# Mixer input normalized before its split, accumulators copied out by ScalarE, weights split by ScalarE and VectorE

## The chip, the cores and the metric

The kernel runs on one core of one Trainium2 chip. The metric is the device time of one execution in microseconds (us), of which the median over several runs is given. The core's engines are TensorE (PE in the profile; its weight loads are PEld), VectorE (DVE), ScalarE (ACT), GpSimd (POOL) and SyncE (SP), which issues the transfers. Each works through its own queue in order.

## The reference

One step of a decoder layer over 1024 prompt positions and 8 decode positions, 1032 rows of 1024 features. The mixer projects the normalized input once; the columns are q, k and v of three attention patterns, the gate z, the convolved inputs xBC and dt of a state space branch. Both branches go through one output projection, and a SwiGLU block follows.

```python
def rmsnorm(x, w):
    xf = x.astype(jnp.float32)
    y = xf * lax.rsqrt(jnp.mean(xf * xf, axis=-1, keepdims=True) + NORM_EPS)
    return (y * w.astype(jnp.float32)).astype(x.dtype)
...
    qkv, z, xbc, dt_raw = split_mix(xn @ w_in)
...
    mix = jnp.concatenate([attn.astype(xn.dtype), ssm.astype(xn.dtype)], axis=-1) @ w_out
...
    yp = yp + rmsnorm(mix, norm_mix_post[l])
    yp = yp + rmsnorm(swiglu(rmsnorm(yp, norm_ffn_pre[l]), w_ffn_in[l], w_ffn_out[l]), norm_ffn_post[l])
```

## The kernel before

Features lie on the 128 partitions (8 tiles of 128, index `k`), the 1032 rows on the free axis in three chunks of 344 (`CH`). Every product is made of parts in TensorE's fp32r type: an operand `x` is split into a rounded high part `xh` and the rest `xl`, a weight tile into `wh` and `wl`, and `unit` (L161) adds `wh*xh`, `wl*xh` and `wh*xl` over the 8 tiles: 24 matmuls of 344 columns into one accumulator in PSUM. `gemm` (L182) loads one weight tile of 128 output features, runs a unit for each chunk and hands each accumulator to an evacuation function `ev`.

`load_w` (L136) brings a tile of 128 x 1024 weights from HBM (`wr`) and splits it. `wr`, `wh` and `wl` have two buffers each, so a tile's split waits until TensorE has left the tile before the last, and a transfer into `wr` until the low part of the tile before the last is made. The first load is split by GpSimd in quarters (L146, L148). The others go to GpSimd (L156, L158), but for four loads of the last chunk of the output projection (`share`, L153, L154), which ScalarE and VectorE split. Some further weights (the attention part of the output projection, one FFN tile, the last FFN group) have splits of their own on ScalarE and GpSimd.

The stages in order of time: the mixer's input; xBC columns (`w_in` tiles 44 to 55) with a convolution, and dt (to some 200 us); then q, k, v columns of the three patterns (`proj_raw`, L580) with attention beside the state space scan, and scores against the caches (200 to 900); z columns and the gate, with the merge of the patterns (L844 to L858) and the values of the caches (L861 to L889) beside them; the output projection and two norms (to some 1210); the FFN in four groups of hidden tiles; the last norm.

The mixer's input (L200 to L233) is only scaled by the norm's weights before the split: ScalarE writes `xh` from the loaded chunk `xc` with one scaled copy (L217), VectorE makes `xl` (L218). The row scale `rin`, one over the root mean square, is worked out beside the products: squares on ScalarE (L228), their sum over `k` on VectorE or GpSimd (L230), one product with a matrix of ones (L232) and `rms` (L190): a root on ScalarE and a reciprocal on VectorE. As the row scale is the same for all features of a row, it is multiplied in when an accumulator is copied out: `scaled` (L237, the multiplication in L239) on VectorE for xBC (`xb`), dt (`dtT`), q, k, v (`rw`) and z (`zt`). The first two weight tiles run as six units with six accumulators.

Accumulators of the mixer's columns have two slots in PSUM (six for the xBC columns). The order of instructions on each queue is made ahead of time by a scheduler that takes ready instructions by priority: `evac` before `w` (weights) before `side` before `late` before `main` (the matmuls of units). On the chip each queue keeps that order.

Of the kernel before, what the change touches and what calls it, by code (L numbers as in the profile page):

```python
# [48 lines left out]
def trunk(tc, a, o):  # L49
# [86 lines left out]
    def load_w(src, cols, share=False, kind="w"):  # L136
        with prio(kind):
# [5 lines left out]
            if nload[0] == 1:  # L143
                for q in range(4):
                    qs = slice(q * 256, (q + 1) * 256)
                    nc.gpsimd.tensor_scalar(out=wh[:, qs], in0=wr[:, qs], scalar1=1.0, scalar2=0.0, op0=ALU.mult,  # L146
                                            op1=ALU.add)
                    nc.gpsimd.tensor_tensor(out=wl[:, qs], in0=wr[:, qs], in1=wh[:, qs], op=ALU.subtract)  # L148
            elif share == 2:
                nc.scalar.copy(wh[:, :cols], wr[:, :cols])  # L150
                nc.gpsimd.tensor_tensor(out=wl[:, :cols], in0=wr[:, :cols], in1=wh[:, :cols], op=ALU.subtract)
            elif share and nload[0] % 2:
                nc.scalar.copy(wh[:, :cols], wr[:, :cols])  # L153
                nc.vector.tensor_tensor(out=wl[:, :cols], in0=wr[:, :cols], in1=wh[:, :cols], op=ALU.subtract)  # L154
            else:
                nc.gpsimd.tensor_scalar(out=wh[:, :cols], in0=wr[:, :cols], scalar1=1.0, scalar2=0.0,  # L156
                                        op0=ALU.mult, op1=ALU.add)
                nc.gpsimd.tensor_tensor(out=wl[:, :cols], in0=wr[:, :cols], in1=wh[:, :cols], op=ALU.subtract)  # L158
# [43 lines left out]
    # mixer input scaled by its norm's weights, split into two exact parts; its row scale is applied after the product  # L202
    xh = [actp.tile([P, T], F32R, tag="act", name=f"xh{k}") for k in range(KT)]
    xl = [actp.tile([P, T], F32R, tag="act", name=f"xl{k}") for k in range(KT)]
    rin = rowp.tile([P, T], F32, tag="row", name="rin")
    with ExitStack() as ps0:
        xp = pool(ps0, "xp", 3, side="left")
        sp = pool(ps0, "sqp", 3, side="left")
        xcs = []
        cuts = []  # L210
        for c, (c0, c1) in enumerate(CH):
            xc = xp.tile([P, KT, CW], F32, tag="xc", name="xc")
            xcs.append(xc)
            with prio("evac"):
                for k in range(KT):
                    nc.sync.dma_start(out=xc[:, k], in_=a["xT"][k, :, c0:c1])
                    cut = nc.scalar.activation(out=xh[k][:, c0:c1], in_=xc[:, k], func=AF.Copy, scale=nw(MIX_PRE, k))  # L217
                    nc.vector.scalar_tensor_tensor(out=xl[k][:, c0:c1], in0=xc[:, k], scalar=nw(MIX_PRE, k),  # L218
                                                   in1=xh[k][:, c0:c1], op0=ALU.mult, op1=ALU.subtract)
            cuts.append(cut)  # L220
            if c == 0:
                first.append(load_w(a["w_in"][45], 1024, kind="evac"))
        for c, (c0, c1) in enumerate(CH):
            acc = sp.tile([P, CW], F32, tag="acc", name="acc0")
            with prio("w"):
                for k in range(KT):
                    sq = acc if k == 0 else sp.tile([P, CW], F32, tag=f"sq{c % 2}", name="sq")
                    after(nc.scalar.activation(out=sq, in_=xcs[c][:, k], func=AF.Square), cuts[c])  # L228
                    if k:
                        (nc.vector if c == 1 else nc.gpsimd).tensor_tensor(out=acc, in0=acc, in1=sq, op=ALU.add)  # L230
                ssq = side_ps("ssq")
                nc.tensor.matmul(ssq[:, :CW], ones, acc, start=True, stop=True)  # L232
                rms(ssq[:, :CW], rin[:, c0:c1])  # L233
# [68 lines left out]
    # xBC columns, causal convolution  # L302
# [4 lines left out]
    for m in range(12):  # L307
# [4 lines left out]
        def ev(c, ps, xb=xb):  # L312
            c0, c1 = CH[c]
            return scaled(xb[:, 3 + c0:3 + c1], ps, c, rin)
# [46 lines left out]
    # dt: both parts of the weights side by side, then token-major  # L361
# [4 lines left out]
    for c, (c0, c1) in enumerate(CH):  # L366
# [5 lines left out]
        with prio("evac"):  # L372
            scaled(dtT[:, c0:c1], ps[:32], c, rin)
# [10 lines left out]
    with prio("side"):  # L384
# [43 lines left out]
        # decode step of the state space branch  # L428
# [44 lines left out]
    # chunked scan of the state space branch  # L473
    hst = sc.tile([P, 2, 512], F32, name="hst")

    def ssd(c, g):
# [42 lines left out]
        # outputs with features on partitions, two heads on each tile  # L519
# [36 lines left out]
    # y kept with its decode columns for the gate  # L556
    with prio("side"):
        nc.sync.dma_start(out=y_d[:, :, S:T].rearrange("k p b -> p k b"), in_=yd)
    # attention
# [20 lines left out]
    def proj_raw(mt):  # L580
        rw = rawp.tile([P, T], F32, tag="raw", name="rw")

        def ev(c, ps, rw=rw):
            c0, c1 = CH[c]
            return scaled(rw[:, c0:c1], ps, c, rin)
# [43 lines left out]
    def attend(g, hp, qr, kr, vt):  # L629
        nh = nhp.tile([P, S], F32, tag="nh", name="nh")  # L630
        for j in range(8):
# [43 lines left out]
            # features on partitions, the two heads side by side in the array  # L675
# [45 lines left out]
    # attention of the decode tokens over the caches  # L721
# [8 lines left out]
    def dec_scores(g):  # L730
        nc.vector.tensor_tensor(out=prod[:, g], in0=dec[0][:, g].rearrange("p h b -> p (h b)"),
                                in1=dec[1][:, g].rearrange("p h b -> p (h b)"), op=ALU.mult)
        # rows of the decode tokens: q for the scores, k and v for the new cache rows
# [79 lines left out]
    # merge of the three patterns by their softmax denominators  # L813
# [46 lines left out]
    # values of the caches  # L860
# [31 lines left out]
    # z columns and the gate  # L892
# [4 lines left out]
    for k in range(KT):  # L897
        zt = gp.tile([P, T], F32, tag="zt", name="zt")

        def ev(c, ps, zt=zt):  # L900
            c0, c1 = CH[c]
            return scaled(zt[:, c0:c1], ps, c, rin)
# [34 lines left out]
    # output projection: state space part, its row scale applied after the product  # L937
# [46 lines left out]
    # output projection: attention part, then both norms around the residual  # L984
# [57 lines left out]
    # SwiGLU in groups of hidden tiles  # L1042
# [23 lines left out]
    def ffn_in(ts, order):  # L1066
        """hidden tiles ts; order: (tile, chunk) one after the other"""
# [24 lines left out]
    def ffn_out(gi):  # L1092
# [15 lines left out]
        # the last group chunk by chunk, its weights and the residual on chip  # L1108
# [40 lines left out]
        for c, (c0, c1) in enumerate(CL):  # L1149
# [5 lines left out]
            with prio("side"):  # L1155
                for m in range(KT):
# [7 lines left out]
                    # two tiles to a transfer, in columns that have gone out  # L1164
# [8 lines left out]
    for gi, (t0, t1) in enumerate(groups):  # L1173
        if gi == 0:
            # the last chunk of the first two tiles late, while its norms are under way
# [98 lines left out]
```

## Time and profile before

| | |
|---|---|
| median of 3 runs | 1947.85 us (1947.51 to 1948.57) |
| span of the profiled execution | 1955.3 us |
| TensorE busy | 1827.1 us (93%) |
| VectorE busy | 1071.0 us (55%) |
| GpSimd busy | 856.4 us (44%) |
| ScalarE busy | 549.2 us (28%) |
| TensorE's granted clock, mean | 0.970 |

The profiled execution took a little longer than the runs that are timed. Busy time of TensorE counts matmuls with their modelled ends, which overlap, so it says that the engine had work, not that it ran at its peak. The granted clock is the share of full speed that TensorE was given: 1.00 is 2.4 GHz, 0.50 is 1.2 GHz, a mean between them is a mixture. A wait is put down to the instruction that released it last. In the rows, `L158` is line 158 of the kernel, `wl<-wr,wh` names what is written from what, and `g` is an accumulator.

### The profile page before, as it was taken

The page shows a single profiled execution, that of the slowest core. Times are in us where ns is not written, and L with a number is a line of the kernel's source. Part 1 is how long each engine was busy: PE and PEld are TensorE (multiplying, and loading weights), DVE is VectorE, ACT ScalarE, POOL GpSimd, SP SyncE. Part 2 cuts the span into 40 slices and gives each one's busy share as a digit, 9 for nine tenths or more (in the row PEclk, how much of TensorE's full clock was granted, in tenths as well). Part 3 has the DMA queues.
Part 4 walks back from the last instruction along what each step waited for, and adds up shares of the span by engine and source line. Part 5 has one row for each costly group of instructions (what it writes and reads, how often), then busy time and mean ns, then how long its engine had stood idle before and what let it go on. Part 6 is the DMA issues. An engine that isn't in the chain of part 4 may idle for free.

```text
span 1955.3 us, 29265 instructions
## 1 busy us (share of the span) xinstructions
PE 1827.1 (93%) x11685; PEld 1712.4 (88%) x11685; DVE 1071.0 (55%) x1917; ACT 549.2 (28%) x1084; POOL 856.4 (44%) x557
## 2 busy tenths in 40 slices
PE   7999989999999999998789889999999999999994
PEld 7998777888887898886678879999999999999993
DVE  7866776768774554556884796330233223321348
ACT  5322344343533344452231334111111001100142
POOL 6332356665435534356755564223223332233325
PEclk9999999999999999999889999999999999999997
DMA  5322333443324433365554444236533753355362
GB/s 188 114 92 87 111 110 100 126 127 110 117 83 153 161 99 104 130 233 150 154 158 130 134 134 151 97 128 244 178 108 103 253 172 119 119 202 196 116 251 87
DMA packets 125545, 275.27 MB, mean 141 GB/s; under 512 B 17616, under 2 KB 83632, under 8 KB 124000
## 3 DMA queue, kind: packets, MB, share of 16 engines
q1 hardware_dynamic: 125408, 273.39, 42.8%
q8 instruction: 92, 1.51, 0.3%
q14 instruction: 45, 0.37, 0.1%
HBM read 235.86 MB, written 125.47 MB: 185 GB/s over the span
## 4 chain that ended last, share of the span: by engine, by line
PE 39%; DVE 7%; DMA 2%; issue 1%; POOL 1%; ACT 1%; DVEq 0%; SPq 0%; POOLq 0%; ACTq 0%
PE g L169 14%; PE pu L169 12%; PE pg L169 12%; DMA nt<-n_d 1%; DVE mix L1030 1%; DVE fl L1033 1%; PE g L954 1%; DVE nt L856 1%; DVE nt L855 1%; DMA xr<-in_xT 0%; DVE mix L1029 0%; POOL nt L854 0%; DVE fr L192 0%; DVE nr L192 0%; DVE sl L924 0%
## 5 line engine op out<-in xcount | busy, mean ns | idle before, releaser
L169 PE MATMUL g<-xh,wh 128*128 128x344 f32 x1344 | 446.0, 332 | 32.4 <-DVE rw L239 12.7
L169 PE MATMUL g<-xl,wh 128*128 128x344 f32 x1344 | 443.2, 330 | 2.8 <-DVE xl L218 2.7
L169 PE MATMUL g<-xh,wl 128*128 128x344 f32 x1344 | 441.9, 329 | 1.9 <-POOL wl L158 1.2
L156 POOL TENSOR_SCALAR wh<-wr 128x1024 fp32r<-128x1024 f32 (+1 forms) x133 | 140.4, 1056 | 674.5 <-PE g L169 355.8
L158 POOL TENSOR_TENSOR wl<-wr,wh 128x1024 fp32r<-128x1024 f32 (+1 forms) x133 | 312.8, 2352 | 9.8
L169 PEld LDWEIGHTS g<-xh,wh 128*128 128x128 f32 x1344 | 258.1, 192 | 46.4 <-issue 14.4
L169 PEld LDWEIGHTS g<-xh,wl 128*128 128x128 f32 x1344 | 258.1, 192 | 11.5 <-issue 7.5
L169 PEld LDWEIGHTS g<-xl,wh 128*128 128x128 f32 x1344 | 258.0, 192 | 11.0 <-issue 6.1
L239 DVE TENSOR_TENSOR u<-pu,rf 128x344 f32<-128x344 f32 x66 | 34.0, 515 | 237.5 <-PE pu L169 237.5
L169 PE MATMUL pg<-fh,wh 128*128 128x344 f32 x504 | 158.8, 323 | 4.9 <-DVE mix L1010 4.9
L169 PE MATMUL pg<-fl,wh 128*128 128x344 f32 x504 | 162.1, 322 | 0.0
L169 PE MATMUL pu<-fl,wh 128*128 128x344 f32 x504 | 161.8, 321 | 0.0
L169 PE MATMUL pg<-fh,wl 128*128 128x344 f32 x504 | 161.4, 320 | 0.0
L169 PE MATMUL pu<-fh,wh 128*128 128x344 f32 x504 | 161.0, 319 | 0.0
L169 PE MATMUL pu<-fh,wl 128*128 128x344 f32 x504 | 160.4, 318 | 0.0
L169 PE MATMUL g<-hl,wh 128*128 128x344 f32 x432 | 137.8, 319 | 0.0
L169 PE MATMUL g<-hh,wl 128*128 128x344 f32 x432 | 137.4, 318 | 0.0
L169 PE MATMUL g<-hh,wh 128*128 128x344 f32 x432 | 137.1, 320 | 0.0
L659 ACT ACTIVATE sm<-sm,ngm 128x128 f32<-128x128 f32 (+1 forms) x192 | 84.9, 443 | 183.5 <-DVE ngm L655 177.2
L1088 ACT CAST hh<-s 128x344 fp32r<-128x344 f32 x66 | 31.7, 480 | 296.6 <-DVE s L1087 296.6
L614 ACT COPY sw<-rw 32x1032 f32<-32x1032 f32 x96 | 101.0, 1052 | 30.5 <-DVE rw L239 29.4
L1085 ACT ACTIVATE s<-s 128x344 f32<-128x344 f32 x66 | 32.5, 492 | 247.6 <-DVE s L239 247.4
(325 smaller groups left out, 3815.9 us busy)
## 6 DMA issues: line engine op xcount, KB each, us to landing
out_skv<-in_cache SPq DMA_DIRECT2D x64, 1023.5 KB, 5.4
wr<-in_w_in SPq DMA_DIRECT2D x56, 512.0 KB, 3.7
wr<-in_w_fin SPq DMA_DIRECT2D x44, 512.0 KB, 3.6
out_skv<-in_cache SPq DMA_DIRECT2D x16, 1022.0 KB, 5.4
wr<-in_w_out SPq DMA_DIRECT2D x24, 512.0 KB, 4.7
wr<-in_w_fout SPq DMA_DIRECT2D x24, 384.0 KB, 3.9
e<-cs_d SPq DMA_DIRECT2D x16, 512.0 KB, 4.1
n_d<-nh SPq DMA_DIRECT2D x12, 512.0 KB, 3.6
```

What stands on the lines that cost most here:

```text
L156: nc.gpsimd.tensor_scalar(out=wh[:, :cols], in0=wr[:, :cols], scalar1=1.0, scalar2=0.0, op0=ALU.mult, op1=ALU.add)
L158: nc.gpsimd.tensor_tensor(out=wl[:, :cols], in0=wr[:, :cols], in1=wh[:, :cols], op=ALU.subtract)
L169: nc.tensor.matmul(ps, x[:, ws], y[:, c0:c1], start=(k == 0 and j == 0), stop=(k == n - 1 and j == 2))
L239: return nc.vector.tensor_tensor(out=dst, in0=ps, in1=r[:dst.shape[0], c0:c1], op=ALU.mult)
L614: nc.scalar.copy(sw[q * 32:(q + 1) * 32, 0:T], rw[s * 32:(s + 1) * 32, :])
L659: nc.scalar.activation(out=sm[:, h, :nk], in_=sm[:, h, :nk], func=AF.Exp, scale=SCALE, bias=ngm[:, g, j, i:i + 1], accum_out=den[:, g, j, ...
L855: nc.vector.tensor_tensor(out=nt[:, 0], in0=nt[:, 0], in1=nt[:, 1], op=ALU.add)
L856: nc.vector.tensor_tensor(out=nt[:, 0], in0=nt[:, 0], in1=nt[:, 2], op=ALU.add)
L954: nc.tensor.matmul(pq[m][c], ws[m][j == 1][:, k * P:(k + 1) * P], (sl if j == 2 else sh)[k][:, CH[c][0]:CH[c][1]], start=(k == 0 and j == ...
L1030: nc.vector.scalar_tensor_tensor(out=mv, in0=mv, scalar=nw(MIX_POST, m), in1=x[:, m % 2], op0=ALU.mult, op1=ALU.add)
L1085: last = nc.scalar.activation(out=s, in_=s, func=AF.Silu)
L1088: nc.scalar.copy(hh[:, c0:c1], s)
```

## The change

Three things change. The mixer's input is normalized fully before the split: the squares of a chunk are summed by eight products with the ones matrix, the row scale of that chunk is worked out, VectorE scales the chunk in place by the norm's weights and the row scale, ScalarE copies it to `xh`, VectorE subtracts for `xl`. The row scale `rin` over all rows is gone, and the accumulators of xBC, dt, q, k, v and z are copied out by ScalarE as they are. All streamed weights except the first load are split by ScalarE (`wh`) and VectorE (`wl`). The splits outside `load_w` stay. Changes of comments are left out here.

```diff
--- before.py
+++ after.py
@@ load_w
             else:
-                nc.gpsimd.tensor_scalar(out=wh[:, :cols], in0=wr[:, :cols], scalar1=1.0, scalar2=0.0,
-                                        op0=ALU.mult, op1=ALU.add)
-                nc.gpsimd.tensor_tensor(out=wl[:, :cols], in0=wr[:, :cols], in1=wh[:, :cols], op=ALU.subtract)
+                nc.scalar.copy(wh[:, :cols], wr[:, :cols])
+                nc.vector.tensor_tensor(out=wl[:, :cols], in0=wr[:, :cols], in1=wh[:, :cols], op=ALU.subtract)
         return wh, wl
@@ trunk, the mixer's input
-    rin = rowp.tile([P, T], F32, tag="row", name="rin")
     with ExitStack() as ps0:
         xp = pool(ps0, "xp", 3, side="left")
         sp = pool(ps0, "sqp", 3, side="left")
-        xcs = []
-        cuts = []
         for c, (c0, c1) in enumerate(CH):
             xc = xp.tile([P, KT, CW], F32, tag="xc", name="xc")
-            xcs.append(xc)
             with prio("evac"):
+                ssq = side_ps("ssq")
                 for k in range(KT):
                     nc.sync.dma_start(out=xc[:, k], in_=a["xT"][k, :, c0:c1])
-                    cut = nc.scalar.activation(out=xh[k][:, c0:c1], in_=xc[:, k], func=AF.Copy, scale=nw(MIX_PRE, k))
-                    nc.vector.scalar_tensor_tensor(out=xl[k][:, c0:c1], in0=xc[:, k], scalar=nw(MIX_PRE, k),
-                                                   in1=xh[k][:, c0:c1], op0=ALU.mult, op1=ALU.subtract)
-            cuts.append(cut)
+                    sq = sp.tile([P, CW], F32, tag="sq", name="sq")
+                    nc.scalar.activation(out=sq, in_=xc[:, k], func=AF.Square)
+                    nc.tensor.matmul(ssq[:, :CW], ones, sq, start=(k == 0), stop=(k == KT - 1))
+                r = sp.tile([P, CW], F32, tag="r", name="r")
+                rms(ssq[:, :CW], r)
+                for k in range(KT):
+                    nc.vector.scalar_tensor_tensor(out=xc[:, k], in0=xc[:, k], scalar=nw(MIX_PRE, k), in1=r,
+                                                   op0=ALU.mult, op1=ALU.mult)
+                    nc.scalar.copy(xh[k][:, c0:c1], xc[:, k])
+                    nc.vector.tensor_tensor(out=xl[k][:, c0:c1], in0=xc[:, k], in1=xh[k][:, c0:c1], op=ALU.subtract)
             if c == 0:
                 first.append(load_w(a["w_in"][45], 1024, kind="evac"))
-        for c, (c0, c1) in enumerate(CH):
-            acc = sp.tile([P, CW], F32, tag="acc", name="acc0")
-            with prio("w"):
-                for k in range(KT):
-                    sq = acc if k == 0 else sp.tile([P, CW], F32, tag=f"sq{c % 2}", name="sq")
-                    after(nc.scalar.activation(out=sq, in_=xcs[c][:, k], func=AF.Square), cuts[c])
-                    if k:
-                        (nc.vector if c == 1 else nc.gpsimd).tensor_tensor(out=acc, in0=acc, in1=sq, op=ALU.add)
-                ssq = side_ps("ssq")
-                nc.tensor.matmul(ssq[:, :CW], ones, acc, start=True, stop=True)
-                rms(ssq[:, :CW], rin[:, c0:c1])
@@ trunk, xBC columns
-            return scaled(xb[:, 3 + c0:3 + c1], ps, c, rin)
+            return nc.scalar.copy(xb[:, 3 + c0:3 + c1], ps)
@@ trunk, dt
-            scaled(dtT[:, c0:c1], ps[:32], c, rin)
+            nc.scalar.copy(dtT[:, c0:c1], ps[:32])
@@ proj_raw (q, k, v)
-            return scaled(rw[:, c0:c1], ps, c, rin)
+            return nc.scalar.copy(rw[:, c0:c1], ps)
@@ trunk, z columns
-            return scaled(zt[:, c0:c1], ps, c, rin)
+            return nc.scalar.copy(zt[:, c0:c1], ps)
```

## Rows read from the trace of the kernel before

**Rows 1.** Page, part 1: busy us, share of the span, instructions.
```profile
PE 1827.1 (93%) x11685; PEld 1712.4 (88%) x11685; DVE 1071.0 (55%) x1917; ACT 549.2 (28%) x1084; POOL 856.4 (44%) x557
```

**Rows 2.** By stage: length, PE, PEld, DVE, ACT, POOL busy, PEclk, DMA, GB/s.
```profile
0.00:200.00 200.00, 186.72 (x1176) 179.76 (x1177) 144.54 (x206) 65.25 (x96) 77.57 (x70) 1.00 0.35 121
200.00:900.00 700.00, 665.35 (x4563) 579.99 (x4562) 451.59 (x1072) 288.75 (x630) 354.11 (x219) 0.98 0.40 126
900.00:1050.00 150.00, 118.29 (x606) 102.05 (x604) 115.96 (x126) 32.03 (x45) 93.49 (x53) 0.88 0.54 153
1050.00:1210.00 160.00, 139.82 (x803) 135.31 (x804) 118.51 (x147) 59.74 (x105) 87.66 (x57) 0.93 0.42 134
1210.00:1900.00 690.00, 690.00 (x4378) 690.00 (x4377) 196.05 (x314) 86.52 (x177) 215.91 (x136) 1.00 0.48 162
```

**Rows 3.** Waits of PE over the span: us in total, times, longest us.
```profile
PE g L169 <- DVE rw L239: 12.7, 6, 4.8
PE g L169 <- DVE zt L239: 12.2, 4, 5.4
PE nps L878 <- DVE cvt L877: 7.9, 3, 4.9
PE g L169 <- POOL wl L158: 6.9, 4, 2.2
```

**Rows 4.** Timeline, first 40 us: start us, us, operation, [idle before <-releaser].
```profile
5.63 4.09 ACT L217 ACTIVATE xh<-xc,par 128x344 fp32r<-128x344 f32 x8 [3.40 <-DMA xc<-in_xT]
6.36 0.62 PE L169 MATMUL g<-xh,wh 128*128 128x344 f32 x1 [6.36 <-POOL wh L146]
14.84 0.42 PE L169 MATMUL g<-xl,wh 128*128 128x344 f32 x1 [1.85 <-DVE xl L218]
27.25 2.03 DVE L218 SCALAR_TENSOR_TENSOR xl<-xc,par,xh 128x344 fp32r<-128x344 f32 x4
33.11 2.29 DVE L192 RECIPROCAL rin<-rin 128x344 f32<-128x344 f32 x1
38.36 0.42 PE L169 MATMUL g<-xh,wl 128*128 128x344 f32 x1 [1.23 <-POOL wl L158]
```

**Rows 5.** Lines 232 and 191: duration ns min/median/max, first and last start us.
```profile
L232 PE MATMUL ssq<-acc,ones x6: 450/451/452, 30.0 to 44.6; 128*128 128x344 f32 x6
L191 ACT ACTIVATE rin<-ssq,epst x3: 533/549/549, 30.9 to 45.0; 128x344 f32<-128x344 f32 x3
```

**Rows 6.** The chain that ended last, in the FFN: start us, us, what.
```profile
1312.05 67.74 PE g L169 x432
```

**Rows 7.** Groups by line and shape: busy us, mean ns | idle before, releaser.
```profile
L158 POOL TENSOR_TENSOR wl<-wr,wh 128x1024 fp32r<-128x1024 f32 x109 | 268.3, 2461 | 7.8
L156 POOL TENSOR_SCALAR wh<-wr 128x1024 fp32r<-128x1024 f32 x109 | 120.4, 1105 | 523.4 <-PE pg L169 261.7 <-PE g L169 253.5 <-PE pu L169 4.0
L154 DVE TENSOR_TENSOR wl<-wr,wh 128x1024 fp32r<-128x1024 f32 x4 | 5.4, 1358 | 0.0
L239 DVE TENSOR_TENSOR rw<-g,rin 128x344 f32<-128x344 f32 x108 | 54.7, 510 | 43.1 <-PE g L169 42.9
L153 ACT CAST wh<-wr 128x1024 fp32r<-128x1024 f32 x4 | 4.2, 1049 | 11.1 <-PE g L169 9.2 <-DMA wr<-in_w_out 2.0
L1103 ACT COPY fac<-g 128x344 f32<-128x344 f32 x24 | 10.7, 447 | 55.7 <-PE g L169 53.3 <-DMA out_skv<-in_cache 2.4
```

**Rows 8.** VectorE lines with two SBUF inputs: duration ns min/median/max.
```profile
L218 DVE SCALAR_TENSOR_TENSOR xl<-xc,par,xh x24: 564/1035/2672, 6.2 to 28.7; 128x344 fp32r<-128x344 f32 x24
L1089 DVE TENSOR_TENSOR hl<-s,hh x66: 516/518/2087, 1194.7 to 1879.6; 128x344 fp32r<-128x344 f32 x66
L855 DVE TENSOR_TENSOR nt<-nt x16: 361/1038/2621, 937.9 to 1046.8; 128x256 f32<-128x256 f32 x16
```

**Rows 9.** Line 158 alone, 900 to 1050 us: length, POOL busy, PEclk, DMA.
```profile
900.00:1050.00 150.00, 24.66 (x10) 0.88 0.54 153
```

**Rows 10.** Waits of ACT over the span: us in total, times, longest us.
```profile
ACT eb L512 <- DMA e<-cs_d: 30.4, 8, 7.8
```

## Prediction

> **What bounds the kernel now.** I read the page's engine shares first, then the busy time by stage, then PE's waits. TensorE is busy 1827 of 1955.3 us, VectorE 1071, GpSimd 856, ScalarE only 549 [rows 1]. The stages differ. From 1210 to 1900 us (the FFN) PE is busy all 690 us at a granted clock of 1.00; 432 matmuls take 67.74 us there, 0.157 us each [rows 2, 6]. Nothing that only relieves another engine can shorten that stretch. The time that PE loses lies elsewhere, in two forms: idle time, and the lower of TensorE's two clock levels (1.2 against 2.4 GHz), which I price as (1 - PEclk) x length. From 200 to 900 us (attention) that is 34.7 idle + 14 clock, from 900 to 1050 (z columns, merge of the patterns, values of the caches) 31.7 + 18, from 1050 to 1210 (output projection, norms) 20.2 + 11 [rows 2]. All that this change can win is a part of these 130 us.
>
> What ends the gaps stands in PE's waits. The largest are PE waiting for an accumulator that VectorE has yet to copy out: 12.7 us on rw (6 waits, attention) and 12.2 on zt (4 waits, z columns). Next come the matmuls over the cache values, 7.9 on VectorE's sums, and weights still in GpSimd's split, 6.9 [rows 3]. VectorE is late for a visible reason: its operations with two SBUF inputs have very uneven durations. L1089 takes 516 ns at least and 518 in the median, but up to 2087; L855 takes 361 to 2621, median 1038 [rows 8]. The evacuation from PSUM stays at 510 ns [rows 7]. I read the long ones as those that run beside GpSimd, which in 900 to 1050 us is busy 93.5 of 150 us [rows 2].
>
> **Splitting the weights on ScalarE and VectorE.** Removed from GpSimd: per load 1.105 + 2.461 = 3.57 us [rows 7]; 133 loads move (only the first stays). Added: 1.05 us on ScalarE and 1.36 on VectorE [rows 7], 2.4 us from start to end. In the FFN, ScalarE is busy 87 and VectorE 196 of 690 us [rows 2]; a hidden tile is 6 units of 24 matmuls (6 x 24 x 0.157 = 22.6 us) and needs two splits, of which the nearer has one unit, 3.77 us, to finish in. The cover there is PE's own unit: 3.57 fitted in it, so 2.4 does. I price the FFN at 0; if the cover failed, 2 splits x 22 tiles would each show what exceeds 3.77. SP's queue, which holds back the next weight DMA until the low part is made, is released about 1.1 us sooner; nothing waits longer for it.
>
> In 900 to 1050 us ten low parts took 24.7 us on GpSimd [rows 9], with their high parts (10 x 1.105) 35.7 of the 93.5 busy: 38% of what stretches VectorE goes away. VectorE gets ten of 1.36 back. Queued behind such a subtraction are VectorE's merge and gate operations. It waits for ScalarE's copy, which waits for PE to leave the old buffer, but it is needed only a whole tile of weights later (3 units, 11.3 us), so I price the new wait at 0 and keep 1.4 us per load as its upper price.
>
> The Trainium skill (GPSIMD Engine Reference, section Specifications) says that GpSimd and VectorE share SBUF interfaces, and that VectorE instructions with two SBUF inputs or in a two-port mode suffer by it. That agrees with L1089 and L855 against L239 [rows 7, 8]. It speaks against this change in one respect: the low part is itself such an instruction, and GpSimd keeps its other work. If each were stretched as far as L855's longest (2.62 against 1.36), ten of them would cost VectorE 13 us more in that stage; by the median row it is nothing like that.
>
> **Copying out on ScalarE.** 168 evacuations (56 weight tiles x 3 chunks) leave VectorE at 0.51 us each, 86 us in all, and cost ScalarE 0.447 (L1103, the same shape) [rows 7], 75 us. With the splits, ScalarE rises from 549 to some 760 us, 39% of the span. What counts is not length but the queue: an accumulator is now released by an engine that in 900 to 1050 us is busy 32 of 150 us, and no more by one busy 116 [rows 2]. There are two accumulator slots here, so a finished one may wait one unit (3.77 us) at no cost. Behind the evacuation on ScalarE stand the exponentials, rotary copies and SiLU, and it stands behind them: their waits become PE's. This new wait is not in the trace; its lower bound is a gain of all 12.7 + 12.2 us of rw and zt waits, its upper bound is the second rival's price.
>
> **Normalizing ahead of the split.** Now the first product starts at 6.36 us, after one ScalarE scaling, and the row scale is worked out beside it [rows 4]. Changed, chunk 0 needs eight squares (as the eight scalings, 5.63 to 9.72 us [rows 4]), eight products with the ones matrix, a root and a reciprocal. One such product is two records of 0.451 us [rows 5]; how far they overlap the row doesn't tell. Hidden behind the squares they end near 10.6; at the lower clock level, 8 x 0.9 us and more from 6.1, near 14. I take 12.5. Root 0.55 [rows 5], reciprocal 2.29 [rows 4]: VectorE starts to scale at 15.3. From there VectorE paces PE: per tile and chunk one scaling (four in 2.03 us with 0.56 for the last, so 0.49 a step [rows 4, 8]) and one subtraction (0.52 at most [rows 8]), 24 of them: 24.2 us. Two more reciprocals make 4.6, the low part of the second weights 1.4. That ends at 45.5. PE's own work for these six units, 144 x 0.157 = 22.6 us, is covered by it. The third weights can't be split until the first leave their buffers (two of each): 2.4 us, or one unit of 3.77, whichever comes last. So PE reaches the third weight tile near 48.5, against 38.36 now [rows 4]: +10. Removed with it: the additions of squares (14 on GpSimd, 7 on VectorE) and the scaling by the row scale, all beside other work, 0. PE is busy 186.7 of the first 200 us at a clock of 1.00, and 6.4 of the 13.3 idle lie before its first product [rows 2, 4]: nothing after the start has room to give the 10 us back. Bounds: +6 (products hidden, short steps), +16 (slow products, 0.56 + 0.52 a step).
>
> **The sum.** Attention: the rw waits are 12.7 of 34.7 idle; with their share of the clock loss (14 x 12.7 / 34.7 = 5) 18 us. I take half, -9: ScalarE has waits of its own there, but VectorE is less stretched. 900 to 1050: zt (10 of the 12.2), half of the weight waits (3) and 38% of the cache waits (3) are 16 of 31.7 idle; with the same half of the 18 us of clock, 25. I take -20, since VectorE gains subtractions. 1050 to 1210: the other half of the weight waits and its clock share, -5. Start +10, FFN and tail 0. Sum -24. The sum is made against the profiled span of 1955.3, which lies 7.5 above the median of the runs shown, 1947.85; taken off that it gives 1924.
>
> **Rivals.** *ScalarE becomes the queue that holds PE* (slower). Place: attention, 200 to 900 us, 108 evacuations. ScalarE waits there for DMA (30.4 us in 8 waits, the longest 7.8 [rows 10]) and for VectorE's part of the softmax. An evacuation queued behind such a wait outlasts the 3.77 us of cover. Price: a stall as now, 12.7 / 6 = 2.1 us and 0.9 of clock, 3 us; if one evacuation in six meets one, 18 x 3 = 54 instead of 18 now, +36 in place of -9. Sum +21 to the span: 1969. It decides the sign from 11 stalls instead of six, if the rest holds. Against it: ScalarE is idle 411 of these 700 us [rows 2].
>
> *The gaps aren't these engines' to give back* (about no change). GpSimd keeps rotary, merge and softmax-side work, PE's queue order is fixed, so a matmul in it goes on waiting for whatever VectorE does last; only the weight waits (6.9, with clock 10) go. Sum 10 - 10: 1948, between 1940 and 1956.
>
> *TensorE's clock falls in the starved start.* A gap of 1.85 us there left the granted clock at 1.00 [rows 2, 4]. At the lower level a step doubles to 0.31, six products a tile take 1.9 us against VectorE's 1.0, and the start costs +20 instead of +10: 1934. The Trainium skill (TensorE: Matmul & The Clock Gate, Part 1) has the clock fall when the engine is idle too long; the row is against it, as the pace leaves PE mostly busy.
>
> *The merge stage becomes bound by PE alone:* its whole 50 us come back instead of 20: 1895.
>
> **How the numbers follow.** Forecast 1924 with a range of its own of 1908 to 1940 (start +6 to +16, gains 18 to 46): 0.48. ScalarE's queue 0.22, no change 0.18, clock 0.04, merge 0.08. The range 1902 to 1969 takes in the forecast's and the second case whole, and leaves out the far part of the slow case and most of the merge case. A difference under 0.2%, 3.9 us, is about what a measurement of this kernel can't tell from none. Faster: 0.48 + 0.08 + 0.04 + 0.04 of the second case = 0.64; same 0.09; slower 0.27.
>
> **What would show it.** Right: the third weight tile starts near 48 us; L1089's longest falls towards its 516 ns; no PE wait on zt in 900 to 1050; PE still full in the FFN. Wrong: PE waits on rw and zt named with ScalarE and as long as VectorE's now; weight waits named with the low part on VectorE; PE idle in the FFN (3.77 us no longer covers the split); or a start far from +10.

## The result and the profile after

| | before | after |
|---|---|---|
| median of the runs, us | 1948.21 (1947.51 to 1954.35, 4 runs) | 1928.21 (1922.17 to 1929.59, 4 runs) |
| ratio, 95% interval | | 0.9878 (0.9862 to 0.9894) |
| span of the profiled execution, us | 1955.3 | 1927.8 |
| VectorE / ScalarE / GpSimd busy, us | 1071 / 549 / 856 | 1014 / 739 / 394 |

The changed kernel is faster by 1.2%: 20.0 us by the medians, 27.5 by the two profiles. The profile of before lay some 7 us above its median, so a difference of two profiles below may be that much too large. The page's first part (engine, busy us, share, instructions), against [rows 1]:

```profile
PE 1825.0 (95%) x11727; PEld 1709.3 (89%) x11727; DVE 1014.0 (53%) x1896; ACT 739.2 (38%) x1388; POOL 394.5 (20%) x277
```

TensorE's busy time is nearly unchanged; what shrank is the time around it. The same stages as in [rows 2] (length, PE, PEld, DVE, ACT, POOL busy, PEclk, DMA, GB/s):

```profile
0.00:200.00 200.00, 190.82 (x1159) 179.54 (x1160) 107.70 (x178) 93.11 (x153) 5.59 (x24) 1.00 0.33 113
200.00:900.00 700.00, 672.32 (x4650) 587.15 (x4649) 418.63 (x1018) 373.53 (x787) 233.13 (x148) 0.99 0.41 130
900.00:1050.00 150.00, 124.16 (x673) 110.24 (x672) 96.40 (x124) 47.83 (x69) 60.85 (x33) 0.92 0.58 160
1050.00:1210.00 160.00, 147.61 (x888) 144.13 (x887) 125.57 (x163) 68.57 (x118) 56.23 (x40) 0.97 0.44 141
1210.00:1900.00 690.00, 685.85 (x4339) 684.93 (x4338) 244.42 (x389) 152.25 (x254) 21.17 (x16) 1.00 0.48 163
```

Fixed windows no longer hold the same work, since everything has shifted. The stages are therefore also measured between landmarks of PE's own timeline:

| stage, from landmark to landmark | before, us | after, us | change |
|---|---|---|---|
| start of the program to the third weight tile | 36.8 | 49.2 | +12.4 |
| to the last product of the q, k, v columns | 796.2 | 779.0 | -17.2 |
| z columns | 148.1 | 142.6 | -5.5 |
| to the end of the output projection | 179.4 | 168.8 | -10.6 |
| gap before the FFN | 5.2 | 0.4 | -4.8 |
| FFN | 711.5 | 709.1 | -2.4 |
| tail | 78.1 | 78.7 | +0.6 |

Waits of PE over the span (us in total, times, longest), against [rows 3]:

```profile
PE sps L636 <- DVE qr L610: 9.9, 5, 3.8
PE nps L869 <- DVE cvt L868: 6.3, 3, 3.2
PE g L168 <- ACT zt L893: 5.5, 2, 3.9
PE g L168 <- DVE wl L157: 4.0, 4, 1.6
PE g L168 <- ACT rw L576: 3.3, 5, 1.2
```

The accumulator waits, rw and zt, went from 24.9 us to 8.8 and now name ScalarE. VectorE's part of the split makes PE wait 4.0 us in four times.

The start, against [rows 4] (start us, us, operation, idle before and releaser), of ScalarE, PE and VectorE in this order:

```profile
8.06 0.49 ACT L214 ACTIVATE sq<-xc 128x344 f32<-128x344 f32 x1 [0.63 <-PE ssq L215]
14.48 0.55 ACT L190 ACTIVATE r<-ssq,epst 128x344 f32<-128x344 f32 x1
...
6.51 13.26 PE L215 MATMUL ssq<-sq,ones 128*128 128x344 f32 x34 [6.51 <-ACT sq L214]
19.35 0.58 PE L168 MATMUL g<-xh,wh 128*128 128x344 f32 x1
50.17 0.43 PE L168 MATMUL g<-xh,wl 128*128 128x344 f32 x1 [0.52 <-DVE wl L157]
...
15.06 2.30 DVE L191 RECIPROCAL r<-r 128x344 f32<-128x344 f32 x1 [1.69 <-ACT r L190]
17.40 3.99 DVE L219 SCALAR_TENSOR_TENSOR xc<-xc,par,r 128x344 f32<-128x344 f32 x8
40.25 3.50 DVE L222 TENSOR_TENSOR xl<-xc,xh 128x344 fp32r<-128x344 f32 x8
```

The first product of the mixer starts at 19.35 us instead of 6.36, and the third weight tile's low part is first used at 50.17 instead of 38.36: 11.8 us later. During the first sum of squares ScalarE waits for PE (0.63 us before the square at 8.06).

### The profile page after: what moved, and what is told of

Its sections match the earlier page's. It is cut to its first block, busy times and chain, and to the rows that moved or that the text cites. A ratio compares the mean times of both kernels' runs of the same rounds, so it can differ in the third digit from the quotient of the medians.

```text
span 1927.8 us, 29260 instructions
## 1 busy us (share of the span) xinstructions
PE 1825.0 (95%) x11727; PEld 1709.3 (89%) x11727; DVE 1014.0 (53%) x1896; ACT 739.2 (38%) x1388; POOL 394.5 (20%) x277
## 5 line engine op out<-in xcount | busy, mean ns | idle before, releaser
L157 DVE TENSOR_TENSOR wl<-wr,wh 128x1024 fp32r<-128x1024 f32 (+1 forms) x133 | 163.0, 1226 | 124.9 <-ACT wh L156 124.7
L156 ACT CAST wh<-wr 128x1024 fp32r<-128x1024 f32 (+1 forms) x133 | 134.4, 1011 | 214.5 <-PE g L168 128.8
L1110 POOL TENSOR_TENSOR ow<-wr,ow 128x512 fp32r<-128x512 f32 x8 | 11.1, 1407 | 674.9 <-ACT ow L1109 674.9
L606 POOL TENSOR_TENSOR sw<-sw,sin 128x1032 f32<-128x1032 f32 x24 | 74.9, 3122 | 247.6 <-ACT sw L605 184.1
```

What stands on the lines that cost most here:

```text
L606: nc.gpsimd.tensor_tensor(out=sw[:, 0:T], in0=sw[:, 0:T], in1=sin, op=ALU.mult)
L1110: nc.gpsimd.tensor_tensor(out=wl, in0=src, in1=wh, op=ALU.subtract)
```

## Experiments

The change has three separable parts, named A, B and C here: A, the input normalized ahead of its split; B, the accumulators copied out by ScalarE; C, the streamed weights split by ScalarE and VectorE. The kernel before needs its row scale at the evacuation, so B without A is not a full kernel: with C it was run leaving the row scale out (bc_plain_evac), alone it was not. All other combinations were run.

Runs came from several chips, on which the kernel before itself took 1948.2 to 1952.0 us. Kernels are therefore compared by their ratios to the runs of before on the same chip, and a difference of two ratios is turned into us with 1948.2. Each such difference is uncertain by some 4 to 6 us. The change's own ratio is 0.9878; its medians alone would give 0.9897.

| kernel | A | B | C | median, us | ratio (95%) |
|---|---|---|---|---|---|
| a_start_alone | x | | | 1957.92 | 1.0060 (1.0037 to 1.0083) |
| ab_gpsimd_split | x | x | | 1952.69 | 1.0018 (1.0004 to 1.0032) |
| c_split_alone | | | x | 1924.34 | 0.9878 (0.9859 to 0.9897) |
| ac_vector_evac | x | | x | 1937.20 | 0.9944 (0.9923 to 0.9964) |
| bc_plain_evac | | x | x | 1914.44 | 0.9819 (0.9800 to 0.9837) |
| after | x | x | x | 1928.21 | 0.9878 (0.9862 to 0.9894) |

**The parts one by one.** The theory was that C pays for everything and A costs what was predicted; the rival, that the evacuations pay, as the waits of [rows 3] had suggested.

ac_vector_evac: the changed kernel with VectorE copying the accumulators out; the line shown is that of q, k and v, and those of xb, dtT and zt are changed in the same way.

```diff
-            return nc.scalar.copy(rw[:, c0:c1], ps)
+            return nc.vector.tensor_copy(rw[:, c0:c1], ps)
```

> The changed kernel with one part undone: the accumulators are copied out by VectorE again (a plain copy, as the input stays normalized ahead). Theory T (GpSimd's splits stretch VectorE; taking them off it is worth about 25 us, the evacuation on ScalarE about 7, the longer start costs 12): 1948 + 12 - 25 = 1935 us, still faster than before. Rival R (the evacuation's queue is what counts: ScalarE's copies are worth 25, the splits 7): 1948 + 12 - 7 = 1953 us, slower than before.

Measured 1937.2 (0.9944): B is worth 12.9 us here.

ab_gpsimd_split: the changed kernel with the splits back on GpSimd.

```diff
-                nc.scalar.copy(wh[:, :cols], wr[:, :cols])
-                nc.vector.tensor_tensor(out=wl[:, :cols], in0=wr[:, :cols], in1=wh[:, :cols], op=ALU.subtract)
+                nc.gpsimd.tensor_scalar(out=wh[:, :cols], in0=wr[:, :cols], scalar1=1.0, scalar2=0.0,
+                                        op0=ALU.mult, op1=ALU.add)
+                nc.gpsimd.tensor_tensor(out=wl[:, :cols], in0=wr[:, :cols], in1=wh[:, :cols], op=ALU.subtract)
```

> The changed kernel with one part undone: the streamed weights are split by GpSimd again. Theory T: 1948 + 12 - 7 = 1953 us, slower than before, and VectorE's lines with two SBUF inputs are uneven again (the FFN's subtraction up to 2 us). Rival R: 1948 + 12 - 25 = 1935 us.

Measured 1952.7, slower than before. A and B without C lose; C is worth 27.3 us here.

c_split_alone: the kernel before with the opposite edit, C alone.

> The kernel before with one part of the change done: the streamed weights are split by ScalarE and VectorE; the start and the scaled evacuation on VectorE stay. Theory T: 1948 - 25 = 1923 us, a little faster than the whole change, with the third weight tile at 38 us. Rival R: 1948 - 7 = 1941 us, as VectorE's queue now carries evacuations and subtractions.

Measured 1924.3: C alone is worth 23.8 us and has the whole change's ratio.

a_start_alone: the changed kernel with the edits of both ac_vector_evac and ab_gpsimd_split, so that only the start differs from before.

> The kernel before with one part of the change done: the mixer's input normalized ahead of its split; weights split by GpSimd, accumulators copied out by VectorE (a plain copy). Both theories: the start's 12 us and nothing else, 1948 + 12 = 1960 us, the third weight tile at 50 us instead of 38. Should it come out near 1948, the 12 us are given back before 900 us and the start is free.

Measured 1957.9: A costs 11.7 us. Two more pairs give about the same: bc_plain_evac against the whole change 11.5 us, c_split_alone against ac_vector_evac 12.9. The delay of the third weight tile was 11.8: nothing shows that the start's time is given back later.

What PE waits for when B is there and C isn't (ab_gpsimd_split, waits of PE over the span):

```profile
PE nps L870 <- DVE cvt L869: 12.7, 2, 8.5
PE g L169 <- POOL wl L158: 6.8, 4, 2.5
PE sps L637 <- DVE mx L643: 6.2, 5, 2.8
PE wtp L833 <- DVE wo L832: 4.9, 3, 3.7
```

rw and zt are gone from this list's head (4.3 us are left of 24.9), and other operations that VectorE finishes late have come in their place: cvt went from 7.9 [rows 3] to 12.7, mx from 0.7 to 6.2, and wo, with 4.9, wasn't on the list before. Taking the accumulators away from VectorE moved the waits more than it removed them.

**Why C pays: the split's length, or GpSimd beside VectorE?** C shortens the split itself and it empties GpSimd. c_gpsimd_reads keeps C and gives GpSimd, after each split, four subtractions on a scratch tile whose result nobody reads, about as long together as the work it had lost (425 us). c_gpsimd_writes gives it 14 fills of the same tile instead (484 us): the queue is as full, but nothing is read. The diff is that of c_gpsimd_reads against c_split_alone; c_gpsimd_writes has `nc.gpsimd.memset(scr, 0.0)` in the place of each subtraction, 1 + 13 times.

```diff
+    scr = const.tile([P, 192], F32, name="scr")
...
-                nc.scalar.copy(wh[:, :cols], wr[:, :cols])
+                cp = nc.scalar.copy(wh[:, :cols], wr[:, :cols])
...
+                after(nc.gpsimd.tensor_tensor(out=scr, in0=scr, in1=scr, op=ALU.subtract), cp)
+                for _ in range(3):
+                    nc.gpsimd.tensor_tensor(out=scr, in0=scr, in1=scr, op=ALU.subtract)
```

> Splits on ScalarE and VectorE as in the run with that part alone (1924), but GpSimd does useless work beside each split: four subtractions of 192 columns on a scratch tile, with two SBUF inputs, about 3.4 us a load, the time its splits took. No one waits for them but GpSimd's own queue. Theory T1 (GpSimd's work beside VectorE is what cost the time, by stretching VectorE and by keeping GpSimd's queue busy): most of the 25 us is lost again, 1940 to 1949, and VectorE's lines with two SBUF inputs are uneven again. Rival T2 (the weights were late because GpSimd's split is slow, 3.6 us against 2.4): the weights stay early, 1924 to 1928.

> The same, but GpSimd's useless work only writes: 14 fills of 192 columns for each split, again some 3 us a load (the trace will tell). T1a (GpSimd's queue being taken is what counts, its rotary and merge operations come later): as slow as the run with reads, 1940 to 1949. T1b (what counts is that its reads stretch VectorE's operations with two SBUF inputs): fills stretch them little, 1924 to 1930, and the FFN's subtraction stays near 0.52 us.

Measured 1951.6 (ratio 1.0018, 1.0004 to 1.0031) and 1934.1 (0.9920, 0.9903 to 0.9937). With the short split in place and GpSimd reading, the gain is gone entirely: the split's own length isn't what pays. Fills cost 8.2 us against c_split_alone (0.9920 - 0.9878), reads 27.3; the fills' time lies between its two expected cases. The page's first part of c_split_alone, c_gpsimd_reads and c_gpsimd_writes:

```profile
PE 1816.2 (94%) x11685; PEld 1704.7 (89%) x11685; DVE 1097.2 (57%) x2050; ACT 675.1 (35%) x1217; POOL 410.8 (21%) x291
```
```profile
PE 1824.8 (94%) x11685; PEld 1709.9 (88%) x11685; DVE 1138.1 (58%) x2050; ACT 671.9 (35%) x1215; POOL 836.3 (43%) x824
```
```profile
PE 1825.1 (94%) x11685; PEld 1707.3 (88%) x11685; DVE 1100.4 (57%) x2050; ACT 670.9 (35%) x1213; POOL 884.6 (46%) x2154
```

VectorE runs the same 2050 instructions in all three. GpSimd's reads make them 41 us longer, its fills 3. Groups of VectorE by line and shape (busy us, mean ns, idle before and releaser), the convolution and the accumulators' evacuation in c_split_alone and then in c_gpsimd_reads:

```profile
L333 DVE SCALAR_TENSOR_TENSOR cv<-xb,par,cv 128x1024 f32<-128x1024 f32 x36 | 45.8, 1279 | 3.4 <-ACT cv L330 3.1
L238 DVE TENSOR_TENSOR rw<-g,rin 128x344 f32<-128x344 f32 x108 | 54.6, 512 | 46.3 <-PE g L168 45.4
```
```profile
L338 DVE SCALAR_TENSOR_TENSOR cv<-xb,par,cv 128x1024 f32<-128x1024 f32 x36 | 51.6, 1447 | 1.4 <-ACT cv L335 1.0
L243 DVE TENSOR_TENSOR rw<-g,rin 128x344 f32<-128x344 f32 x108 | 54.7, 510 | 51.0 <-PE g L172 50.3
```

The line with two SBUF inputs takes 1279 ns alone and 1447 beside reads (1279 again beside the fills). The evacuation, of whose two inputs one lies in PSUM, stays at 510. That is the contention the prediction read from the uneven durations of [rows 8]. The Trainium skill (SBUF — State Buffer, section "SBUF: two separate sides") says that a VectorE instruction with two SBUF inputs meets GpSimd only where GpSimd's operation reads SBUF; the 41 and 3 us agree. The unevenness that T1 expected back in the FFN came only in the mean: its subtraction takes 615 ns beside the reads and 521 beside the fills, but at most 980 and 983.

By the totals, some 19 of the 27.3 us come with the reads and some 8 with the occupied queue alone, behind which GpSimd's own work (rotary, merge) stands. By stage, from PE's own timeline, it looks otherwise:

| kernel | start of the program to the last q, k, v product, us | from there to the FFN, us | FFN and tail, us |
|---|---|---|---|
| before | 833.0 | 332.7 | 789.6 |
| c_split_alone | 829.1 | 307.0 | 788.4 |
| c_gpsimd_reads | 829.8 | 328.3 | 788.3 |
| c_gpsimd_writes | 823.2 | 323.7 | 786.4 |

C's gain lies between the last q, k, v product and the FFN: 25.7 us. There the reads take back 21.3 and the fills, which read nothing, 16.6. The fills' small total contains 5.9 us gained before that stretch, for which no run shows a reason. So where C pays, most of the gain is lost again without any reads. What is shown is that the work on GpSimd costs the time, and not the split's length; how much of it comes by stretching VectorE and how much by delaying GpSimd's own work is open. The substitutes also run at other moments than the real splits: TensorE's granted clock over the z columns is 0.89 with the reads and 0.86 with the fills, against 0.93 before and 0.96 in c_split_alone.

**Which accumulators.** c_scalar_qk_evac has C, and the q and k accumulators copied out plain by ScalarE, with the row scale multiplied once into the rotary tables instead.

```diff
+        nc.vector.tensor_tensor(out=cos, in0=cos, in1=rin, op=ALU.mult)
+        nc.vector.tensor_tensor(out=sin, in0=sin, in1=rin, op=ALU.mult)
...
-            return scaled(rw[:, c0:c1], ps, c, rin)
+            return nc.scalar.copy(rw[:, c0:c1], ps) if plain else scaled(rw[:, c0:c1], ps, c, rin)
```

> Splits on ScalarE and VectorE, the short start kept, and of the evacuations only those of q and k go to ScalarE: their row scale is multiplied into the rotary tables once (two VectorE operations of 1032 columns). The input needn't be normalized ahead for that. From the four runs: the splits alone gave 1924, the evacuation on ScalarE 9 us more with splits there, of which q and k are 72 of 168 and the part in attention: 1916 to 1920 us, faster than the whole change. If the 9 us come from xBC and z, 1924.

Measured 1926.4 (0.9885, 0.9865 to 0.9906) against 1924.3 without it: nothing gained, the theory's 1916 to 1920 missed. The number fits the other case, xBC and z, but the next runs point to v instead. Three more kernels followed up. abc_qk_vector and abc_v_vector are the changed kernel with q's and k's accumulators, or v's, back on VectorE; bc_plain_evac is C with all these accumulators on ScalarE and the old start, leaving the row scale out. The diff is that of abc_qk_vector, where `plain` marks q and k; abc_v_vector has the two copies swapped.

```diff
-            return nc.scalar.copy(rw[:, c0:c1], ps)
+            return nc.vector.tensor_copy(rw[:, c0:c1], ps) if plain else nc.scalar.copy(rw[:, c0:c1], ps)
```

> The changed kernel, with the q and k accumulators (72 of 108 in attention) copied out by VectorE instead of ScalarE; v, xBC, z and dt stay on ScalarE. All evacuations on ScalarE: 1928.2; all on VectorE: 1937.2; the difference lay in the profiles wholly between 163 us and the end of the q, k and v units (679.3 against 665.3 us). If the 9 us come from v's accumulators, which the run with q and k alone on ScalarE had left on VectorE: 1927 to 1930. If they come from q's and k's in this schedule: 1935 to 1938. If they are spread evenly over the three: 1934, as two thirds go back.

> The changed kernel, with the v accumulators (36 of 108 in attention) copied out by VectorE; q, k, xBC, z and dt stay on ScalarE. If the 9 us come from v's: 1935 to 1938. If from q's and k's: 1927 to 1930. If they are spread evenly: 1931, as one third goes back.

> The kernel before, with the weights split by ScalarE and VectorE and every accumulator of the input projections copied out plain by ScalarE; the start is that of before. It leaves out the multiplication of these products by the row scale. If the evacuation gives its 9 us whatever the start is: 1914 to 1917. If the gain exists only with the start of the changed kernel (where attention ran 5 us longer than in the kernel with the splits alone until ScalarE copied out): 1922 to 1926, as with q and k alone on ScalarE.

Measured 1920.7 (0.9846, 0.9826 to 0.9866), 1942.3 (0.9966, 0.9954 to 0.9979) and 1914.4. The first two lie beyond every case expected, in the direction of v's; the third is where a gain that doesn't depend on the start was expected. Against the whole change, which each of the two kernels differs from in one group only, v's accumulators on ScalarE are worth 17.1 us (0.9966 - 0.9878), and q's and k's cost 6.2 (0.9878 - 0.9846). That leaves some 2 of B's 12.9 us for xBC, z and dt, which no run moved by themselves. B's gain is v's, less a little that q and k take back. The same window of attention (200 to 830 us) in ac_vector_evac, abc_v_vector, abc_qk_vector and after:

```profile
200.00:830.00 630.00, 598.82 (x4118) 520.92 (x4117) 423.33 (x1004) 286.79 (x586) 204.19 (x130) 0.97 0.38 120
```
```profile
200.00:830.00 630.00, 596.05 (x4084) 517.17 (x4083) 391.87 (x931) 305.76 (x647) 204.74 (x130) 0.97 0.38 119
```
```profile
200.00:830.00 630.00, 605.66 (x4212) 525.75 (x4211) 412.67 (x994) 305.65 (x637) 207.84 (x131) 0.99 0.38 122
```
```profile
200.00:830.00 630.00, 606.36 (x4212) 527.26 (x4210) 375.16 (x926) 332.94 (x710) 205.39 (x131) 0.99 0.39 122
```

With v on VectorE (the first two) PE is idle 31 to 34 us and its clock is granted at 0.97; with v on ScalarE (the last two) 24 us and 0.99. It isn't a matter of load: abc_qk_vector has more VectorE time in this window than abc_v_vector, and is faster. From the first dt product to the last q, k, v product the two with v on ScalarE take 665, the two with v on VectorE 679 and 684 us.

**The order of the queues.** The scheduler lays the queues out anew for every kernel, so every comparison above measures an edit with the order it brings. abc_k_first changes the order alone: k is projected ahead of q, with the same instructions on the same engines. PE's sequence then differs in 312 lines; between the kernels with v's accumulators on ScalarE and on VectorE it differs in 675.

```diff
-            qr = do_qk(g, hp, 0)
             kr = do_qk(g, hp, 1)
+            qr = do_qk(g, hp, 0)
```

> The changed kernel, with k projected ahead of q for each pair of heads: the same instructions on the same engines, only the order in which the scheduler lays out the queues differs (the sequence of PE's queue differs in 312 lines; between the kernels with v's accumulators on ScalarE and on VectorE it differs in 675). If the order alone is worth little and the differences of 5 to 20 us between the kernels that move q's, k's or v's accumulators are those engines' work: 1926 to 1930. If a new order of the queues is itself worth such amounts: outside 1923 to 1933, on either side.

Measured 1924.0 (0.9853, 0.9837 to 0.9870) on a chip where the kernel before took 1952.0. By the ratios that is 4.9 us under after, with overlapping intervals, and 1919.6 on the scale of the other kernels: outside the wide band, where the second case had put it. The z columns, which the edit doesn't touch, took 128.8 us instead of 142.6, and the stretch from the last q, k, v product to the FFN 304.9 instead of 311.8. So an order may be worth some 5 us by itself, and q's and k's 6 us can't be told from that.

One other order is no bound on what orders can do. A's price is nearly free of this: in the two pairs that give 11.5 and 12.9 us, PE's sequences in the profiles differ in fewer than 100 records. For C and for v's accumulators the stages speak, one profile of each kernel:

- From the last q, k, v product to the FFN, the nine kernels with the splits off GpSimd and nothing in their place take 305 to 315 us, and the five whose GpSimd has the splits or a substitute 322 to 333.
- From the third weight tile to the last q, k, v product, the five kernels with C and v's accumulators on ScalarE take 779 to 782 us, and the four with C, v's on VectorE and nothing put on GpSimd 793 to 799. On each side these are three clearly different orders (over 450 records apart). Without C v's engine makes no difference there: 789.4 us in ab_gpsimd_split, 789.3 in a_start_alone.

**The start.** abc_start_vector_sum adds the first chunk's squares on VectorE and makes one product with the ones matrix instead of eight.

```diff
-                    sq = sp.tile([P, CW], F32, tag="sq", name="sq")
+                    first_sq = c == 0 and k == 0
+                    sq = sp.tile([P, CW], F32, tag="acc" if first_sq else "sq", name="sq", bufs=1 if first_sq else 3)
                     nc.scalar.activation(out=sq, in_=xc[:, k], func=AF.Square)
+                    if c == 0:
+                        if k == 0:
+                            acc = sq
+                        else:
+                            nc.vector.tensor_tensor(out=acc, in0=acc, in1=sq, op=ALU.add)
+                        if k == KT - 1:
+                            nc.tensor.matmul(ssq[:, :CW], ones, acc, start=True, stop=True)
+                        continue
```

> The changed kernel with the squares of the first chunk summed by VectorE (idle there) and one product with the ones matrix instead of eight. If the eight products at the lower clock level held the start (they took to 14.4 us while the squares alone would end near 9.7), the first reciprocal comes near 12 us instead of 15.06 and the third weight tile near 47 instead of 50; if VectorE's own pace sets the start in any case, it moves by the same 3 us; if the later chunks' squares set it, not at all.

Timeline of VectorE and then of PE:

```profile
6.69 5.59 DVE L220 TENSOR_TENSOR sq<-sq 128x344 f32<-128x344 f32 x7 [4.33 <-ACT sq L215]
14.46 2.30 DVE L191 RECIPROCAL r<-r 128x344 f32<-128x344 f32 x1 [1.05 <-ACT r L190]
...
12.33 1.52 PE L222 MATMUL ssq<-sq,ones 128*128 128x344 f32 x2 [12.33 <-DVE sq L220]
49.53 0.42 PE L168 MATMUL g<-xh,wl 128*128 128x344 f32 x1 [0.52 <-DVE wl L157]
```

The reciprocal starts at 14.46 instead of 15.06, the third tile at 49.53 instead of 50.17; a single run took 1924.1 us. The additions take the place of the products, 5.59 us in all. The expected 12 and 47 were missed: the additions end at 12.28, after 0.8 us each in the mean, and the one product with its two records takes another 1.52. What was saved, 0.6 us, reached the third tile whole.

## Why the prediction was right, and where it was not

It said 1924 and faster; the median is 1928.2. The sum of changes was -24; it is -23.8 by the ratio, -20.0 by the medians. The sum held, but two of its terms were wrong in opposite directions; that they nearly cancel is luck.

| term | predicted, us | measured by the pairs of kernels, us |
|---|---|---|
| start (A) | +10 | +11.5 to +12.9 |
| accumulators on ScalarE (B): attention -9, zt's 10/16 of -20 | -21.5 | -8 to -13 |
| splits off GpSimd (C): 6/16 of -20, and -5 | -12.5 | -23 to -27 |

- **The start** held: +11.8 at the third tile, near the middle of its bounds, and A's price in every pair. Its inner steps were off by less. The sum of squares took till 14.48 instead of 12.5, as the squares waited for PE's products in it; VectorE started to scale at 17.40 instead of 15.3. After that VectorE was faster than priced, done at 43.75 (40.25 + 3.50) instead of 45.5, and it no longer paced PE. PE's own work did, for it also held the other two chunks' products with the ones matrix, which had been priced at nothing.
- **The evacuation** is the term that was mis-sized. The step that failed is reading a wait by its name: 12.7 us on rw and 12.2 on zt [rows 3] were credited to the engine that copies out, but when ScalarE did it without C, PE waited for cvt, mx and wo instead. The z columns, where zt's waits had been priced, took 5.5 us less in the change and 8.8 less with C alone (139.3 us): no gain of B shows there. What B has is v's accumulators in attention, where -9 had been priced; the stage gave -17.2, of which up to 7 may be the profile's of before.
- **The splits** were priced by weight waits and a share of the cache waits. VectorE's stretch had been seen, and said to fall by 38%, but no time was given to it except in those waits, and none to GpSimd's own work behind the splits. The stretching is real and did fall. L1089's and L855's successors (ns min/median/max), against [rows 8]:

```profile
L1080 DVE TENSOR_TENSOR hl<-s,hh x66: 500/517/975, 1153.3 to 1851.4; 128x344 fp32r<-128x344 f32 x66
L846 DVE TENSOR_TENSOR nt<-nt x16: 355/424/2597, 928.2 to 1034.0; 128x256 f32<-128x256 f32 x16
```

  The first line's longest fell from 2087 ns to 975 and its median stayed, but it stands in the FFN, where PE hardly gained (709.1 against 711.5 us). The second is the merge, in the stretch where C pays: its median fell from 1038 ns to 424, its longest stayed. That this relief makes up C's gain isn't shown: the fills lengthen VectorE by 3 us in all and lose most of the gain in that stretch. The low part on VectorE, which could have been stretched itself, took 1284 ns in the mean of the 109 large ones, not the 2.62 us of the contrary case.
- **Waits priced at nothing.** PE waits on the low part on VectorE 6.8 us (4.0 at L157, 2.8 at L154), against 9.3 before (6.9 on GpSimd's, 2.4 at L154): most of those waits stayed, where some 9 us (3 of the 16 parts of -20, and -5) had been booked as won.
- **After 900 us** the two stages were to give -25; z, output projection and the gap before the FFN gave -20.9.
- **ScalarE as the queue that holds PE** fell: PE waits for ScalarE on rw 3.3 us in 5 times, the longest 1.2, where the rival needed 18 of 2.1. A trace of it may be in q's and k's evacuations, which are better on VectorE, but by no more than an order of the queues may be worth.
- **The gaps aren't these engines' to give** fell, and with it its premise that PE's order is fixed: the scheduler moved it.
- **The clock in the starved start**: granted 1.00 there, so that rival fell as it was put; its +20 didn't come. **The merge stage bound by PE alone** fell: PE is still idle 25.8 of 150 us at 0.92.
- **Signs and sums.** The sign "no PE wait on zt" wasn't met: two waits, 5.5 us in all and 3.9 at the longest, name ScalarE. Two of the prediction's sums don't come out: a start of +16 with gains of 18 ends the range at 1946 and not at 1940, and the merge case gives 1894 and not 1895. Neither changes the outcome.

The fastest full kernel tried is abc_qk_vector, 1920.7 (0.9846), with abc_k_first (0.9853) too near to tell apart; the splits alone, with the old start, reach 0.9878 with one edit. bc_plain_evac, at 0.9819, shows what is left if the row scale could be applied without delaying the start. How v's accumulators on VectorE lengthen attention by some 19 us was not settled: the longest wait in abc_v_vector is PE's for qr (18.3 us in 3 times, against 10.5 in 3 in abc_qk_vector), but v's own evacuation starts on average only some 0.8 us later after its product than in abc_qk_vector, and the order of the queues changed as well.

## What to carry to other kernels

A wait named after an engine says who came last, not who to relieve: before pricing it as a gain, ask what that engine was slow for. Here one part, taking the weight splits off GpSimd, carried the whole gain, though the waits named VectorE's copies. Look whether lines with two SBUF inputs have a median or a maximum well above their shortest while GpSimd works, and try taking such work off GpSimd by one edit before moving evacuations. Test each part alone: the part with the shortest diff carried the gain, and one of the others cost 12 us. And compare stage by stage: a small total, as the fills' 8 us, can be a gain in one stage and a larger loss in the next.

## What the runs showed of the hardware

- In all, GpSimd's fills hardly lengthen VectorE (+3 us of 1097 beside 484 us of fills), its subtractions do (+41 beside 425 us). The kernel loses 8 and 27 us by them.
- The first products with the ones matrix took 781 to 942 ns a record until 12 us, and 450 to 490 after 18.7, with the granted clock at 1.00 in both stretches. The rows show the longer time and not its cause. The prediction had 8 x 0.9 us and more as the slow case of these products, ending near 14; that is where they ended.
